# First feed-forward's gate vector: from TensorE products at the kernel's begin to weight rows on VectorE, GpSimd and ScalarE behind the first two tiles

## The chip, the cores and the metric

One core of a Trainium2 chip runs the whole program. The metric is the device time of one execution in microseconds (us); less is better. Timed runs are given by their median; one further execution was profiled, and the trace rows are from that one.

## What is computed

The model is a two-layer backbone over 768 tokens (256 context, 512 latent) of width 1024. Each layer has a feed-forward, a mixer and a second feed-forward, each with an adaLN modulation (shift, scale, gate) that is a matrix product with the conditioning vector:

```python
mod   = (silu(c)     @ w_mod + b_mod).reshape(1, 1, 9, 1024)     # for the latent tokens
mod_c = (silu(c_ctx) @ w_mod + b_mod).reshape(1, 1, 9, 1024)     # for the context tokens
h, gt = pre_mod(x, mod, norm_g, 0)       # h = rms_norm(x) * g * (1 + scale) + shift; gt = gate
x  = x  + 0.5 * gt  * swiglu(h,  w_gu, w_down)
xc = xc + 0.5 * gtc * swiglu(hc, w_gu, w_down)
```

The change concerns `gt` and `gtc` of the first feed-forward of layer 0: piece 2 of nine, 1024 columns of `w_mod`, for two vectors (`c` and `c_ctx`).

## The kernel before, in words

All of it is float32 work. A product is made of three TensorE products of halves: a weight tile `raw` is split by ScalarE into a rounded `whi` (line 128, a copy) and by VectorE into the rest `wlo` (line 129, a subtraction); activations have the same two halves (`hh`, `hl`). Tokens lie in the free dimension, so a gate is one number per partition and 128-column block.

The tile framework orders the instructions of each engine when it builds the program: a list schedule by readiness, with program order as the priority. Each engine then runs its queue strictly in that order. `keep_in_program_order` ties an instruction behind the one that was traced before it on its engine; other instructions may still be put between. Pools are taken from the left or right end of SBUF like stacks; with `reuse_waits="tile"` a new tile that covers the place of old ones waits for those tiles alone.

The begin. SP issues nearly all loads in one queue. `first_load` brings 1 MB tiles `m` (tag `m0`, 4 buffers) of `w_mod0a`: eight tiles with shift and scale of one 128-block each, then four tiles with the gate's columns. `first_product` multiplies a tile with silu(c) on TensorE (line 208, 16 instructions), ScalarE copies the row out (line 211), and four small products (line 214) turn it into columns; VectorE adds the bias (lines 221 to 224, for the gate line 230). Each of the eight shift and scale tiles lets `norm_apply` make one 128-block k of `h` (lines 348 to 351).

Meanwhile TensorE works on the first two tiles of the hidden layer, f = 0 and 1 (line 506, in the order k, f): 192 matmuls in three PSUM tiles. Then `up` takes them out (SiLU on ScalarE, product with the PSUM half on VectorE, split). f = 2 and 3 follow with `pair` (line 375). From f = 4 on a Strassen-like scheme with seven half-size products per tile is used (`unit`, line 607, matmuls of 384 columns). It needs sums of blocks of `h`: `seven_open` makes them on VectorE (lines 577 and 565), four times for k = 0 to 3: sums in two buffers `tt`, and from these the split tiles `t` (T1, T2, T4; eight tiles in the pool `tsum`, on the right side, 36 KB of each partition) and `t3`, later split into h (T3). Each `unit` also makes weight sums on VectorE (line 629) and splits them; these halves are named S1 to S4 here. The other modulation pieces are made later by `mod_step` from weight rows on VectorE (line 298, one row tile `wm` of 128x512 for two instructions), with silu of the conditioning row, broadcast over the partitions, in `cb` (lines 276 and 277).

The right side holds first the pool `w2` (the split weights of f = 0 and 1, 32 KB), which is closed after the two tiles; `tsum` takes its place. The gate `mod[0][2]` is first used at line 401 after six hidden tiles.

Of the kernel before, what the change touches and what calls it, by code (L numbers as in the profile page):

```python
# [8 lines left out]
F32 = mybir.dt.float32  # L9
F32R = mybir.dt.float32r  # L10
BF16 = mybir.dt.bfloat16
I32 = mybir.dt.int32
U8 = mybir.dt.uint8
AF = mybir.ActivationFunctionType
ALU = mybir.AluOpType
# [3 lines left out]
D = 1024  # L19
KT = D // 128  # L20
# [27 lines left out]
class Net:  # L48
# [146 lines left out]
        nc.vector.reduce_sum(self.four, self.ident.rearrange("p (j v) -> p v j", j=4)[:, 0:2, :], axis=AX.X)  # L195

    def first_load(self, m, pool):
        raw = pool.tile([128, KT, 256], F32, tag="m0", name="m0", bufs=4)
        self.nc.sync.dma_start(out=raw, in_=self.ins["w_mod0a"][m])
        return raw  # L200

# [21 lines left out]
        nc.vector.tensor_scalar(out=sc, in0=scale, scalar1=b[:, KT + m:KT + m + 1], scalar2=1.0, op0=ALU.add, op1=ALU.add)  # L223
        nc.vector.tensor_scalar(out=sc, in0=sc, scalar1=self.ng[0][:, 0, m:m + 1], scalar2=None, op0=ALU.mult)

    def first_gate(self, pool, i, raw):

        for j, x in enumerate(self.first_product(pool, raw)):
            m = 2 * i + j
            self.nc.vector.tensor_scalar(out=self.mod[0][2][:, m, :], in0=x, scalar1=self.bmod[0][:, 2 * KT + m:2 * KT + m + 1],  # L230
                                         scalar2=0.5, op0=ALU.add, op1=ALU.mult)

    def first_stats(self, pool):

# [222 lines left out]
    def ffn(self, l, sub, idx, segs, nxt, bg=(0, 0), first=4, start=False):  # L457
        nc = self.nc
        gate = self.mod[l][3 * sub + 2]
        gu = self.ins[f"gu{l}{idx}"]  # L460

        w2s = ExitStack()
        w2 = self.pool("w2", w2s, side="right")
        early = 2
        w = {}
        for f in range(2):
            w[f] = self.load_split(gu[f], 2048, w2)
            yield False
        h = yield True
        st = ExitStack()  # L470
        with st:
            pool = self.pool("ffn", st)
            hid = {}

            def hidden(f):
                hid[f] = (pool.tile([128, T], F32R, tag="dh", name="dh", bufs=6),
                          pool.tile([128, T], F32R, tag="dl", name="dl", bufs=6))

            def up(f, ss, regs=None):

                if not regs:
                    regs = self.regions(ss)
                    self.pair(w[f], KT, h, ss, regs)
                if f not in hid:
                    hidden(f)
                sg = pool.tile([128, T], F32, tag="sg", name="sg", bufs=1)
                for reg, (s0, s1) in zip(regs, ss):
                    nc.scalar.activation(out=sg[:, s0:s1], in_=reg[0], func=AF.Silu)
                    nc.vector.tensor_tensor(out=sg[:, s0:s1], in0=sg[:, s0:s1], in1=reg[1], op=ALU.mult)
                a, b = ss[0][0], ss[-1][1]  # L490
                self.split(sg[:, a:b], hid[f][0][:, a:b], hid[f][1][:, a:b])

            main = [(0, CTX), (CTX, T)] if segs[0][0] == 0 else [(CTX, T)]
            if start:

                a = [self.psum_a() for _ in range(3)]
                a = a[1:] + a[:1]
                for f in range(2):
                    nc.tensor.matmul(out=a[2][:, f, :], lhsT=self.zero[:, 0:128], rhs=self.zero, start=True, stop=False)
                regs = [[[a[2][:, f, j * 256:(j + 1) * 256] for j in range(2)], [a[f][:, j, :] for j in range(2)]]  # L500
                        for f in range(2)]
                for f, k in [(f, k) for k in range(KT - 2) for f in range(2)] + [(f, KT - 2 + k) for f in range(2) for k in range(2)]:
                        for j in range(2):
                            for i, (wi, xi) in enumerate(((0, 0), (0, 1), (1, 0))):
                                for s, (s0, s1) in enumerate(main):
                                    nc.tensor.matmul(out=regs[f][s][j], lhsT=w[f][j][wi][:, k * 128:(k + 1) * 128],
                                                     rhs=h[k][xi][:, s0:s1], start=(s == 1 and k == 0 and i == 0),
                                                     stop=(k == KT - 1 and i == 2 and s + j > 0))
                for f in range(2):
                    up(f, main, regs[f])  # L510
            else:
                for seg in segs:
                    for f in range(early):
                        up(f, [seg])
                    if seg == segs[0]:
                        w[early] = self.load_split(gu[early], 2048)
                        up(early, [seg])
            w2s.close()
            sts = ExitStack()
            seven_start, seven = self.seven_open(sts, h, segs[0][0])  # L520
            if not start:
                up(early, [(segs[1][0], T)])
                early += 1
            for pi, (f0, nf) in enumerate(PARTS):
                for f in range(f0, f0 + nf):
                    if f >= early:
                        if f >= first:
                            if f == first:
                                sp = seven_start()
                                if self.pending:  # L530
                                    self.mod_open(self.pool("modp", sts, side="right"))
                            hidden(f)
                            sg = pool.tile([128, T], F32, tag="sg", name="sg", bufs=1)
                            seven(sp, gu[f], sg, hid[f])
                        else:
                            w[f] = self.load_split(gu[f], 2048)
                            up(f, main)
                    if f >= first:
                        self.mod_step(bg[0])
                xk = [hid[f] for f in range(f0, f0 + nf)]  # L540
                dn = self.ins[f"dn{l}{idx}_{nf}"][pi % 2 if nf == 6 else pi - 2]
                load = lambda u: self.load_split(dn[u], 2 * nf * 128)
                if pi == len(PARTS) - 1:
                    self.mod_step(1000)
                    sts.close()
                    self.psum_open()
                    h = self.close_out(load, nf, xk, segs, gate, nxt)
                else:
                    for u in range(4):
                        wd = load(u)  # L550
                        regs = self.regions(main)
                        self.pair(wd, nf, xk, main, regs)
                        self.add_gated(regs, u, main, gate)
                        self.mod_step(bg[1])
        yield h
# [1132 lines left out]
def build(tc, ins, outs, stages=("ffn1_0", "pair", "ffn2_0", "ffn1_1", "gla", "ffn2_1")):  # L1688
    with ExitStack() as ctx:
        n = Net(tc, ctx, ins, outs)  # L1690
# [11 lines left out]
        with ExitStack() as st:  # L1702
            pool = n.pool("start", st)
            l, sub, segs = first[stages[0]]
            h = n.h_new()
            n.first_open(pool)
            n.x_move(ins["x_t"], False, [(0, T)])
            if stages[0] == "ffn1_0":
                raw = {}
                for m in range(2):  # L1710
                    raw[m] = n.first_load(m, pool)
                    gens[0].early()
                with tc.high_priority():
                    bc = n.first_stats(pool)
                for m in range(2):
                    n.first_norm(pool, m, raw[m])
                for m in range(KT):
                    if m > 1:
                        n.first_norm(pool, m, n.first_load(m, pool))
                    for s0, s1 in ((0, CTX), (CTX, T)):  # L1720
                        n.norm_apply(pool, 0, 0, (s0, s1), bc[:, s0:s1], m, h)
                for i in range(4):
                    n.first_gate(pool, i, n.first_load(KT + i, pool))
            else:
                for m in range(KT):
                    n.first_norm(pool, m, n.first_load(m, pool))
                n.mod_queue(*[(0, p) for p in range(2, 9)], *[(1, p) for p in range(9)])
                with tc.tile_pool(name="mm", bufs=1) as mp:
                    n.mod_open(mp)
                    n.mod_step(1000)  # L1730
                gens[0].early(9)
                for seg in segs:
                    n.norm_mod(pool, l, sub, seg, h)
# [114 lines left out]
```

## Time and profile before

| | |
|---|---|
| Timed runs, median of 3 (lowest to highest) | 2703.78 us (2703.27 to 2707.57) |
| Profiled execution | 2706.87 us, of which the span of the profile is 2705.1 us |
| Mean granted TensorE clock | 0.991 of full speed |
| Busy in the span | TensorE matmul 97%, VectorE 80%, ScalarE 44%, GpSimd 6% |

The span runs from the first to the last instruction that the profile shows. PE is TensorE, PEld its weight loads, DVE VectorE, ACT ScalarE, POOL GpSimd, SP the engine that issues the DMAs. An engine's busy share is a mean over stages; what a microsecond is worth is read from the stage it is in.

### The profile page before, as it was taken

The numbers are of one execution on the slowest core, as the hardware profiler recorded it, in microseconds if no ns is written. First come the engines' busy times: TensorE is split into PE (matmuls) and PEld (weight loads), VectorE is DVE, ScalarE is ACT, GpSimd is POOL, SyncE is SP. The second block draws the span as 40 slices with busy tenths as digits, with TensorE's granted clock in tenths as the row PEclk, the third lists the DMA queues.
The fourth block names the chain that finished last, engine by engine and source line by source line (L and its number), as shares of the span: only waits on it lengthen the run. The fifth ranks groups of instructions, "written<-read, shape, count | busy, mean of one in ns | idle before, by whom it ended". The sixth has DMA issues, their size and how long they took to land. (4 is left out here: it accounts for less than half of the span.)

```text
span 2705.1 us, 44031 instructions
## 1 busy us (share of the span) xinstructions
PE 2616.4 (97%) x16800; PEld 2433.8 (90%) x16800; DVE 2163.0 (80%) x4503; ACT 1197.2 (44%) x2254; POOL 171.6 (6%) x206
## 2 busy tenths in 40 slices
PE   7999999999879899999999999999999999999999
PEld 5899999989767789999999899999998998989898
DVE  6789798977888867797988878888777777768777
ACT  4324242445757744242424542424345565435344
POOL 0000000013543200000000000000000121000000
PEclk9999999999989999999999999999999999999999
DMA  8143444331000140434343314343232111422333
GB/s 314 42 150 115 139 133 144 122 128 42 24 24 1 44 144 28 129 113 129 118 140 100 117 63 137 104 147 107 93 109 92 60 67 63 148 71 92 105 106 125
DMA packets 103572, 279.31 MB, mean 103 GB/s; under 512 B 12256, under 2 KB 15200, under 8 KB 101824
## 3 DMA queue, kind: packets, MB, share of 16 engines
q1 hardware_dynamic: 103360, 276.50, 31.5%
q8 instruction: 132, 2.16, 0.3%
q14 instruction: 80, 0.66, 0.1%
HBM read 269.11 MB, written 7.34 MB: 102 GB/s over the span
## 5 line engine op out<-in xcount | busy, mean ns | idle before, releaser
L128 ACT ACTIVATE whi<-raw 128x512 fp32r<-128x512 f32 (+3 forms) x466 | 355.5, 767 | 740.5 <-PE r L375 331.3
L129 DVE TENSOR_TENSOR wlo<-raw,whi 128x512 fp32r<-128x512 f32 (+3 forms) x466 | 401.0, 863 | 81.8 <-ACT whi L128 78.7
L607 PE MATMUL r<-t,whi 128*128 128x384 f32 (+1 forms) x1704 | 400.8, 323 | 1.5 <-DVE u L644 0.9
L607 PE MATMUL r<-hh,wlo 128*128 128x384 f32 (+1 forms) x1136 | 366.0, 322 | 0.0
L607 PE MATMUL r<-hh,whi 128*128 128x384 f32 (+1 forms) x1136 | 365.8, 322 | 0.0
L607 PE MATMUL r<-hl,whi 128*128 128x384 f32 (+1 forms) x1136 | 365.8, 322 | 0.0
L298 DVE SCALAR_TENSOR_TENSOR junk<-wm,cb 128x512 bf16<-128x512 f32 x480 | 329.5, 686 | 12.7 <-ACT cb L277 7.7
L607 PEld LDWEIGHTS r<-t,whi 128*128 128x128 f32 x1704 | 295.7, 188 | 2.8 <-DVE u L644 1.8
L607 PE MATMUL r<-t,wlo 128*128 128x384 f32 (+1 forms) x852 | 273.3, 323 | 0.0
L375 PE MATMUL r<-dh,whi 128*128 128x512 f32 (+1 forms) x952 | 267.4, 346 | 0.8 <-ACT whi L128 0.8
L375 PE MATMUL r<-dh,wlo 128*128 128x512 f32 (+1 forms) x952 | 266.7, 346 | 0.3 <-DVE wlo L129 0.3
L375 PE MATMUL r<-dl,whi 128*128 128x512 f32 (+1 forms) x952 | 266.8, 344 | 0.0
L128 ACT ACTIVATE whi<-s 128x512 fp32r<-128x512 f32 x284 | 174.7, 625 | 180.9 <-DVE s L629 67.3
L607 PEld LDWEIGHTS r<-hl,whi 128*128 128x128 f32 x1136 | 213.4, 188 | 0.8
L607 PEld LDWEIGHTS r<-hh,wlo 128*128 128x128 f32 x1136 | 213.4, 188 | 0.4 <-DVE wlo L129 0.4
L607 PEld LDWEIGHTS r<-hh,whi 128*128 128x128 f32 x1136 | 213.3, 188 | 0.3
L375 PEld LDWEIGHTS r<-dh,wlo 128*128 128x128 f32 x952 | 178.6, 188 | 24.4 <-DVE wlo L129 1.1
L375 PEld LDWEIGHTS r<-dh,whi 128*128 128x128 f32 x952 | 178.0, 188 | 24.5 <-ACT whi L128 2.7
L375 PEld LDWEIGHTS r<-dl,whi 128*128 128x128 f32 x952 | 178.1, 188 | 23.4
L129 DVE TENSOR_TENSOR wlo<-s,whi 128x512 fp32r<-128x512 f32 x284 | 190.9, 685 | 3.8 <-ACT whi L128 3.2
L401 DVE SCALAR_TENSOR_TENSOR x<-r,mod,x 128x512 f32<-128x512 f32 (+1 forms) x168 | 100.1, 632 | 90.9 <-PE r L375 90.5
L607 PEld LDWEIGHTS r<-t,wlo 128*128 128x128 f32 x852 | 159.9, 188 | 0.1
(417 smaller groups left out, 5847.3 us busy)
## 6 DMA issues: line engine op xcount, KB each, us to landing
raw<-gu SPq DMA_DIRECT2D x176, 512.0 KB, 3.8
wm<-w_mod SPq DMA_DIRECT2D x240, 256.0 KB, 2.9
raw<-dn SPq DMA_DIRECT2D x88, 320.0 KB, 3.0
raw<-dn SPq DMA_DIRECT2D x64, 384.0 KB, 3.1
raw<-w_out SPq DMA_DIRECT2D x28, 512.0 KB, 3.9
m<-w_mod0a SPq DMA_DIRECT2D x12, 1024.0 KB, 10.3
raw<-w_in SPq DMA_DIRECT2D x8, 512.0 KB, 4.9
raw<-w_kq SPq DMA_DIRECT2D x8, 512.0 KB, 3.6
```

The costliest lines, as they stand in the source:

```text
L128: self.nc.scalar.activation(out=hi, in_=src, func=AF.Copy)
L129: (e or self.nc.vector).tensor_tensor(out=lo, in0=src, in1=hi.bitcast(F32), op=ALU.subtract)
L298: nc.vector.scalar_tensor_tensor(out=junk, in0=w, scalar=1.0, in1=self.cb[:, v, :], op0=ALU.mult, op1=ALU.mult, accum_out=self.acc[:, m, v ...
L375: m = nc.tensor.matmul(out=outs[s][j], lhsT=w[j][wi][:, k * 128:(k + 1) * 128], rhs=xk[k][xi][:, s0:s1], start=(k == 0 and i == 0), stop=( ...
L401: self.nc.vector.scalar_tensor_tensor(out=self.xs[m][:, s0:s1], in0=regs[s][j], scalar=gate[:, m, v:v + 1], in1=self.xs[m][:, s0:s1], op0= ...
L607: nc.tensor.matmul(out=o, lhsT=y[wi], rhs=x[k][xi], start=first and k == 0 and i == 0, stop=last and k == H - 1 and i == 2, skip_group_che ...
```

## The change

The four gate products at the begin go away: no `first_load` of the four gate tiles, no `first_product` on them, no line 230. `m0` has 3 buffers in place of 4, and a pool `gate` (19 KB of each partition) is opened on the right side ahead of `w2`. After the first two hidden tiles `first_gate` computes the same vector: silu of both conditioning rows, broadcast; then for each of the eight 128-blocks m and both halves i of the contraction a 256 KB row tile `w` (3 buffers), one VectorE multiply with sum for `c`, one GpSimd multiply for `c_ctx`, and one ScalarE copy with sum over GpSimd's product. `mod_finish` adds the bias and the factor 0.5. The VectorE, ScalarE and SP instructions are tied behind the ones traced before them.

```diff
     def first_load(self, m, pool):
-        raw = pool.tile([128, KT, 256], F32, tag="m0", name="m0", bufs=4)
+        raw = pool.tile([128, KT, 256], F32, tag="m0", name="m0", bufs=3)
...
+    def first_gate(self, pool, l=0, p=2):
+        nc, H, keep = self.nc, D // 2, self.tc.keep_in_program_order
+        cb = [pool.tile([128, 2, H], F32, name=f"gc{i}") for i in range(2)]
+        for i in range(2):
+            for v in range(2):
+                src = self.ins["c_row"][v:v + 1, i * H:(i + 1) * H]
+                keep(nc.sync.dma_start(out=cb[i][:, v, :], in_=src.to_broadcast([128, H])))
+        for i in range(2):
+            keep(nc.scalar.activation(out=cb[i], in_=cb[i], func=AF.Silu))
+        acc = [pool.tile([128, KT, 2], F32, name=f"ga{i}") for i in range(2)]
+        for m in range(KT):
+            for i in range(2):
+                w = pool.tile([128, H], F32, tag="gw", name="gw", bufs=3)
+                keep(nc.sync.dma_start(out=w, in_=self.ins[f"w_mod{l}"][p * KT + m][:, i * H:(i + 1) * H]))
+                junk = pool.tile([128, H], BF16, tag="gj", name="gj", bufs=1)
+                keep(nc.vector.scalar_tensor_tensor(out=junk, in0=w, scalar=1.0, in1=cb[i][:, 0, :], op0=ALU.mult,
+                                                    op1=ALU.mult, accum_out=acc[i][:, m, 0:1]))
+                t = pool.tile([128, H], F32, tag="gt", name="gt", bufs=2)
+                nc.gpsimd.tensor_tensor(out=t, in0=w, in1=cb[i][:, 1, :], op=ALU.mult)
+                keep(nc.scalar.activation(out=t, in_=t, func=AF.Copy, accum_out=acc[i][:, m, 1:2]))
+        nc.vector.tensor_tensor(out=self.mod[l][p], in0=acc[0], in1=acc[1], op=ALU.add)
+        self.mod_finish(l, p)
...
-        w2s = ExitStack()
+        gs, w2s = ExitStack(), ExitStack()
+        if start:
+            gp = self.pool("gate", gs, side="right")
         w2 = self.pool("w2", w2s, side="right")
...
                 for f in range(2):
                     up(f, main, regs[f])
+                w2s.close()
+                self.first_gate(gp)
+                gs.close()
...
-                for i in range(4):
-                    n.first_gate(pool, i, n.first_load(KT + i, pool))
```

## Rows read from the trace of the kernel before

**Rows 1.** The page's first part: busy us, share, instructions of each engine.

```profile
PE 2616.4 (97%) x16800; PEld 2433.8 (90%) x16800; DVE 2163.0 (80%) x4503; ACT 1197.2 (44%) x2254; POOL 171.6 (6%) x206
```

**Rows 2.** Stretches: from:to length, busy of PE PEld DVE ACT POOL, PE clock, DMA, GB/s.

```profile
57.81:82.80 24.99, 24.99 (x175) 18.38 (x175) 6.28 (x18) 3.27 (x8) 0.00 (x0) 1.00 0.03 12
...
80.79:121.42 40.63, 40.63 (x235) 36.27 (x234) 35.45 (x57) 18.09 (x30) 0.00 (x0) 1.00 0.14 46
```

**Rows 3.** Timeline of PE around a gate product: start, duration, instruction.

```profile
63.10 0.63 PE L208 MATMUL b<-m,silu_T 128*32 128x256 f32 x6
63.66 0.61 PE L214 MATMUL b<-four,m0r 128*128 128x2 f32 x4
64.19 1.05 PE L208 MATMUL b<-m,silu_T 128*32 128x256 f32 x10
65.18 0.62 PE L506 MATMUL a<-hh,whi 128*128 128x256 f32 x2
```

**Rows 4.** Timeline of PE, first matmuls of f = 2, f = 4, and the fourth product.

```profile
82.80 0.28 PE L375 MATMUL b<-hh,whi 128*128 128x256 f32 x1
...
116.25 0.33 PE L607 MATMUL r<-hh,whi 128*128 128x384 f32 x1
...
122.48 0.34 PE L607 MATMUL r<-hh,whi 128*128 128x384 f32 x1
```

**Rows 5.** Timeline of DVE, in brackets idle time before and its releaser.

```profile
80.79 1.82 DVE L577 TENSOR_TENSOR tt<-hh,hl 128x768 f32<-128x768 f32 x2
...
90.79 0.95 DVE L129 TENSOR_TENSOR dl<-sg,dh 128x768 fp32r<-128x768 f32 x1
...
93.73 1.14 DVE L565 TENSOR_TENSOR tt<-tt 128x384 f32<-128x384 f32 x2
...
119.20 0.69 DVE L129 TENSOR_TENSOR wlo<-raw,whi 128x512 fp32r<-128x512 f32 x1 [2.50 <-ACT whi L128]
...
120.74 0.68 DVE L129 TENSOR_TENSOR wlo<-s,whi 128x512 fp32r<-128x512 f32 x1
```

**Rows 6.** Timeline of ACT, the first split of a sum and silu of cb.

```profile
83.70 0.53 ACT L128 ACTIVATE t<-tt 128x384 fp32r<-128x384 f32 x1 [0.55 <-DVE tt L565]
...
117.59 1.06 ACT L277 ACTIVATE cb<-cb 128x1024 f32<-128x1024 f32 x1 [2.21 <-DMA cb<-c_row]
```

**Rows 7.** Timeline of DVE, two row products of the later modulation.

```profile
163.35 0.69 DVE L298 SCALAR_TENSOR_TENSOR junk<-wm,cb 128x512 bf16<-128x512 f32 x1
...
164.09 0.69 DVE L298 SCALAR_TENSOR_TENSOR junk<-wm,cb 128x512 bf16<-128x512 f32 x1
```

**Rows 8.** Groups by form on POOL and ACT: count, busy us, mean ns, idle before.

```profile
L1008 POOL TENSOR_TENSOR qa<-qa,rs 128x512 f32<-128x512 f32 x6 | 6.2, 1062 | 1.4 <-DVE rs L151 1.4
...
L1091 ACT ACTIVATION_READ_ACCUMULATOR pr<-s,nm 128x1 f32 x96 | 19.6, 204 | 0.0
```

**Rows 9.** Timeline of DVE and POOL together, in the mixer of layer 0.

```profile
797.13 2.05 POOL L1008 TENSOR_TENSOR qa<-qa,rs 128x512 f32<-128x512 f32 x2 [0.20 <-DVE rs L151]
...
798.14 0.28 DVE L1095 TENSOR_TENSOR pt<-t,pt 128x128 fp32r<-128x128 f32 x1
...
804.13 0.28 DVE L707 TENSOR_TENSOR qa<-ra,rb 128x128 f32<-128x128 f32 x1
804.28 2.09 POOL L1008 TENSOR_TENSOR qa<-qa,rs 128x512 f32<-128x512 f32 x2 [0.66 <-DVE rs L151]
804.33 1.14 DVE L708 TENSOR_TENSOR qa<-rb,ra 128x128 f32<-128x128 f32 x1
```

**Rows 10.** DMA: m tiles (KB each, us to landing); landing of row tiles wm.

```profile
m<-w_mod0a SPq DMA_DIRECT2D x12, 1024.0 KB, 10.3
...
DMA to landing us min/median/max: 2.4/2.9/5.3
```

**Rows 11.** Timeline of PE, 256-column matmuls early and ten us later.

```profile
31.29 0.41 PE L506 MATMUL a<-hh,whi 128*128 128x256 f32 x1
...
41.92 0.28 PE L506 MATMUL a<-hh,wlo 128*128 128x256 f32 x1
```

More of the change, by code (lines that the diff above doesn't have):

```diff
@@ L224, in first_norm @@
         nc.vector.tensor_scalar(out=sc, in0=sc, scalar1=self.ng[0][:, 0, m:m + 1], scalar2=None, op0=ALU.mult)
[L226 to L231, printed above, removed]
+    def first_gate(self, pool, l=0, p=2):
[20 more added lines that the diff above has]
+        self.mod_finish(l, p)
     def first_stats(self, pool):
```

## The prediction

> **What bounds the kernel now.** I read the busy shares first, then the waits, then the begin on the timeline, engine by engine. TensorE is busy for 97% of the span [rows 1], so what counts is whether TensorE gets its next operand in time. From 57.81 to 82.80 us, the second half of the first two tiles, it is busy without a gap, and the four gate products lie in there; DMA is nearly silent (0.03) and VectorE mostly idle (6.28 of 24.99 us busy) [rows 2]. A microsecond of TensorE work removed there is a microsecond saved there. From 80.79 to 121.42 TensorE is gapless too, but now VectorE is busy 35.45 of 40.63 us [rows 2]: it makes the sums T1 to T4 and the first weight sums, which the Strassen products at 116.25 and after want [rows 4]. The reader is to see that the change takes work from an engine that has none to spare there, and puts work on another one just where that has little to spare.
>
> I call E the end of line 506, 82.80 before [rows 4], and count from it.
>
> **What is removed.** Between two line 506 matmuls one gate costs TensorE 63.10 to 65.18 us, 2.08 us: sixteen line 208 matmuls in two lots and four of line 214 [rows 3]. The restart of the stream adds something; I take 0.1. Four gates: 4 x 2.2 = 8.8 us (8.3 with no restart cost, 9.1 with 0.2). Their loads (4 MB) end before this stretch [rows 2], the line 211 copies and line 230 adds sit on idle engines: nothing more is saved. E moves to 74.0.
>
> **m0 with three buffers.** Each of the eight remaining tiles is asked for one product later. DMA share is 0.03 after 57.81 [rows 2], and four tiles of 1 MB no longer stand in the queue: I take 0; without that cover it is a tile's landing, 10.3 us in the full queue of before [rows 10].
>
> **What is added on SP and DMA.** Twenty issues: four broadcasts of 256 KB and sixteen rows of 256 KB. The first seven are queued behind the last m tile and land under line 506. The other thirteen wait for a buffer. Behind a waiting issue in SP's queue stand the weights of f = 4 and 5, loaded long ahead; a row lands 2.9 us after its issue [rows 10].
>
> **What is added on VectorE.** The first multiply is tied behind the last VectorE instruction of `up(1)`, at 90.79 before, 8 us after E [rows 5]; the new silu is tied in the same way on ScalarE. So the idle VectorE time ahead of E is out of reach, and all sixteen fall in the busy stretch. Two such instructions start 0.74 us apart, accumulator read included [rows 7]: 16 x 0.74 = 11.8 us, and four small adds, estimated at 0.2, give 12.6 us.
>
> **What is added on GpSimd.** Sixteen 128x512 multiplies; the nearest rows have 1.06 us each [rows 8], 16 x 1.06 = 17.0 us. The question is whether they run beside VectorE. At 804.13 a 128x128 VectorE instruction with both inputs in SBUF takes 0.28 us; the like one at 804.33, just after GpSimd began a 1.04 us multiply, takes 1.14, GpSimd's time more. At 798.14 one whose input is in PSUM takes 0.28 under a running GpSimd multiply [rows 9]. So a GpSimd multiply and a VectorE instruction with two SBUF inputs exclude each other. Nearly all VectorE work of this stretch has two SBUF inputs (lines 577, 565, 129, and the new multiplies). Bounds: 0 if every multiply finds VectorE waiting anyway, 17.0 if none does. VectorE will be the late engine with hardly a gap, so I take 16.6, sixteen at the 1.04 of the undisturbed case.
>
> The Trainium skill (SBUF — State Buffer, Who interferes with whom) says it as a rule: a VectorE instruction with two SBUF inputs contends with a GpSimd instruction that reads SBUF, and the later one blocks fully. This trace agrees (0.28 to 1.14 us [rows 9]); by a reading in which the engines do not disturb each other the 16.6 us would be 0.
>
> **What is added on ScalarE.** Two silus at 1.06 [rows 6] and sixteen copies with sum, each about 0.63 (a copy of 384 columns takes 0.53 [rows 6]) and 0.20 for the sum [rows 8]: 15.4 us. It is busy 18 of 40.63 us [rows 2]; I take 0 of its own. Its splits get later by up to one copy, 0.8 us, a few times.
>
> **Where the stall goes.** `tsum` lies where `w2` was: its first split runs at 83.70, once line 506 is through [rows 6]. Now the gate pool lies at the outer end of the right side and `tsum` (36 KB) covers it too (19 KB): by the order of allocation the tile t11 and all of k = 2 and 3 wait for gate tiles that are read up to the last row. So the sums cannot overtake the gate; they follow it.
>
> The last operand with little slack is S3: its rest is made at 120.74 to 121.42 [rows 5], TensorE wants it at 122.48 [rows 4]: slack 1.1 us. VectorE idles 40.63 - 35.45 = 5.2 us on the way [rows 2], of which 2.5 wait for the silu of cb [rows 5], whose load waits for the place of the sums and comes again; 2.7 can be filled. TensorE is late by 12.6 + 16.6 - 2.7 - 1.1 = 25.4 us. Nothing later gives it back, TensorE having no gaps.
>
> **Sum:** 25.4 - 8.8 = +16.6 us. The span of 2705.1 becomes 2721.7; the execution around it, 2706.87, becomes 2723.5. That execution lay 3.1 us over the median of the runs, so for the median: 2703.8 + 16.6 = 2720.4, say 2720 us. Against no change, 0.2% (5.4 us) is about what a measurement of this kernel tells.
>
> Unknown, for the range: after such a stall the clock. Matmuls of 256 columns took 0.41 us at 31.29, after mostly waiting, and 0.28 at 41.92 [rows 11], the levels of 1.2 and 2.4 GHz. Some 3 to 4 us at the lower level would cost about 2 us, if VectorE isn't the limit then anyway.
>
> **The rivals.**
>
> *GpSimd hides, the waits remain.* If GpSimd runs beside VectorE, three row buffers set the pace: per three rows a landing of 2.9, a multiply of 1.06 and some 0.4 of hand-over, 1.45 us a row, 23 us for sixteen. The gate ends 31 us after E; then one leftover of 1.5, and k = 2 and 3 at 2 x 0.91 + 4 x 0.57 + 1.5 = 5.6 us of VectorE each [rows 5] with some waits, T3 and the weight sums 4: S1 at E + 48.5. Before, TensorE wanted it one product after 116.25, (122.48 - 116.25) / 3 = 2.1 us [rows 4], so at E + 35.5. Late by 13, net +4 to +6: 2709 us. For it: VectorE idles between rows. Against it: [rows 9].
>
> *Only VectorE's own work counts.* No wait for places, no block by GpSimd: 12.6 - 2.7 - 1.1 = 8.8 late, net 0: 2704.
>
> *Rows come too late.* A buffer is free only when both multiplies are done. If the three come free together, three rows take 3 x 1.8 + 2.9 + 0.3 = 8.6 us rather than 5.4, 46 us in all, 17 more: 2737. For it: in the sum a row is wanted 2 x 1.8 = 3.6 us after its buffer is free, and landing takes 3.2. Against it: they come free one by one.
>
> *Faster.* The multiplies are in truth spread so that the sums are done by the time TensorE asks; the whole 8.8 us stay: 2695. For it: `first_gate` isn't wanted until after six tiles, far behind. It decides if VectorE is late by less than the 3.8 us that it can fill, which four of the sixteen rows alone use up; against it stands the tie behind `up(1)` with program order as priority.
>
> **How the numbers follow.** Forecast 0.53 (2715 to 2726). GpSimd hides 0.20, of this 0.16 beyond 0.2% slower and 0.04 within, since it ends at the bound and any latency adds. Rows too late 0.13. VectorE's own work alone 0.08, within. Faster 0.06. Slower 0.53 + 0.16 + 0.13 = 0.82, same 0.12, faster 0.06. The range 2708 to 2733 leaves out faster, the same of 2704 and the upper half of the late rows, 0.2.
>
> **What would show it.** E at 74 (72 to 76) and no line 208 after the eighth tile. The gate's VectorE multiplies start 7 to 9 us after E and end some 28 us later. GpSimd multiplies or VectorE's line 577, 565 and 129 instructions are stretched beyond their 1.06, 0.91 and 0.57 us. No split into `t` for k = 2 and 3 before the last row. TensorE has a gap of 20 us and more ahead of the first Strassen products or in f = 3, ended by VectorE. Wrong would be: a gap under 9 us (then faster); VectorE durations unchanged (then the first rival); VectorE idle with row loads as the releaser (the third).

## The result and the profile after

The kernel with the change takes 2725.86 us (median of 6 runs, 2724.17 to 2731.32), the kernel before, on the same chip, 2705.91 us (6 runs, 2703.27 to 2708.24). The ratio is 1.0078 (95% interval 1.0068 to 1.0089): 20 us slower, where 2720 was forecast (16.6 us slower). The profiled execution has a span of 2726.5 us.

The page's first part, which answers to [rows 1]; the columns are busy us, share and instructions of each engine:

```profile
PE 2611.6 (96%) x16720; PEld 2435.2 (89%) x16720; DVE 2185.6 (80%) x4531; ACT 1208.1 (44%) x2284; POOL 199.7 (7%) x222
```

TensorE does less and the program takes longer, so TensorE must wait somewhere. Its timeline shows what is gained and what is lost, beside [rows 4]:

```profile
73.64 0.28 PE L393 MATMUL b<-hh,whi 128*128 128x256 f32 x1
...
107.54 0.34 PE L630 MATMUL r<-hh,whi 128*128 128x384 f32 x1
...
109.45 0.34 PE L630 MATMUL r<-hh,wlo 128*128 128x384 f32 x1
136.31 1.01 PE L630 MATMUL r<-t,whi 128*128 128x384 f32 x2 [26.52 <-ACT whi L128]
```

E, the end of line 506 and first matmul of f = 2, is at 73.64 and not at 82.80: 9.16 us gained. The first Strassen product, the only one that needs no sum, begins 8.7 us sooner too. Then TensorE stands for 26.52 us until a weight sum is split: the second product needs T1 and S1. The stretches from E to past the gap, with the columns of [rows 2]:

```profile
73.64:112.52 38.88, 36.15 (x205) 31.46 (x203) 35.04 (x48) 20.23 (x47) 27.81 (x16) 1.00 0.31 102
112.52:137.00 24.48, 0.69 (x2) 0.50 (x2) 22.98 (x41) 9.45 (x17) 0.00 (x0) 0.50 0.03 7
137.00:140.00 3.00, 3.00 (x11) 2.97 (x11) 1.90 (x3) 0.50 (x1) 0.00 (x0) 0.58 0.96 266
```

In the first stretch VectorE and GpSimd work on the gate; in the second GpSimd is silent, VectorE works through the sums with hardly a pause (busy 22.98 of 24.48 us), and TensorE has work only at the very end. The third column from the right is the granted clock: 0.50 (1.2 GHz) in the gap, 0.58 in the three microseconds after it.

What the gate's tiles did, one row tile `gw` and the products `gt` (duration min/median/max in ns, first and last start):

```profile
L243 DVE SCALAR_TENSOR_TENSOR gj<-gw,gc x16: 691/1550/1776, 80.5 to 111.9; 128x512 bf16<-128x512 f32 x16
L246 POOL TENSOR_TENSOR gt<-gw,gc x16: 1417/1744/2268, 80.5 to 109.8; 128x512 f32<-128x512 f32 x16
...
DMA to landing us min/median/max: 2.4/2.6/6.9
```

VectorE's multiply, 0.69 us in [rows 7], has a median of 1.55; GpSimd's, some 1.04 in [rows 9], 1.74. On VectorE's timeline the last multiply, with no GpSimd instruction left beside it, is back at 0.69, and the first sum's rest follows it:

```profile
84.48 2.30 DVE L129 TENSOR_TENSOR wlo<-raw,whi 128x1024 fp32r<-128x1024 f32 x1
...
110.11 1.75 DVE L243 SCALAR_TENSOR_TENSOR gj<-gw,gc 128x512 bf16<-128x512 f32 x1
...
111.90 0.69 DVE L243 SCALAR_TENSOR_TENSOR gj<-gw,gc 128x512 bf16<-128x512 f32 x1
...
113.28 0.55 DVE L129 TENSOR_TENSOR t<-tt,t 128x384 fp32r<-128x384 f32 x1
...
134.03 0.96 DVE L129 TENSOR_TENSOR t<-tt,t 128x768 fp32r<-128x768 f32 x1 [0.91 <-ACT t L128]
134.91 0.68 DVE L652 TENSOR_TENSOR s<-raw 128x512 f32<-128x512 f32 x1
```

And ScalarE: the first split of a sum into `t` (k = 0, both parts in one row) stands right behind the gate's last copy. Before, it ran 0.9 us after E [rows 6]; now 38.3 us after it.

```profile
111.34 0.63 ACT L247 ACTIVATE gt<-gt 128x512 f32<-128x512 f32 x1 [0.82 <-POOL gt L246]
111.88 0.19 ACT L247 ACTIVATION_READ_ACCUMULATOR gt<-gt 128x1 f32 x1
111.97 1.24 ACT L128 ACTIVATE t<-tt 128x384 fp32r<-128x384 f32 x2
...
133.16 0.84 ACT L128 ACTIVATE t<-tt 128x768 fp32r<-128x768 f32 x1 [1.48 <-DVE tt L588]
```

So the order of events is: gate from E + 6.8 to E + 39.0, then the rest of the sums and their splits for all four k in 21.6 us (113.28 to 134.91), then the first weight sums, then TensorE. Nearly the whole loss is in this one stage: the first instruction of line 401 (now line 419), which follows it, is 20.2 us late, the last one of the kernel 21.4. The first one on VectorE's timeline, before and after:

```profile
154.49 0.75 DVE L401 SCALAR_TENSOR_TENSOR x<-r,mod,x 128x512 f32<-128x512 f32 x1 [2.15 <-PE r L375]
174.71 0.75 DVE L419 SCALAR_TENSOR_TENSOR x<-r,mod,x 128x512 f32<-128x512 f32 x1 [2.15 <-PE r L393]
```

### The profile page after: what moved, and what is told of

Its sections match the earlier page's. It is cut to its first block, busy times and chain, and to the rows that moved or that the text cites. A ratio compares the mean times of both kernels' runs of the same rounds, so it can differ in the third digit from the quotient of the medians.

```text
span 2726.5 us, 43999 instructions
## 1 busy us (share of the span) xinstructions
PE 2611.6 (96%) x16720; PEld 2435.2 (89%) x16720; DVE 2185.6 (80%) x4531; ACT 1208.1 (44%) x2284; POOL 199.7 (7%) x222
## 5 line engine op out<-in xcount | busy, mean ns | idle before, releaser
L630 PE MATMUL r<-t,whi 128*128 128x384 f32 (+1 forms) x1704 | 402.2, 324 | 28.5 <-ACT whi L128 26.5
```

The lines of the kernel that those rows point to most:

```text
L630: nc.tensor.matmul(out=o, lhsT=y[wi], rhs=x[k][xi], start=first and k == 0 and i == 0, stop=last and k == H - 1 and i == 2, skip_group_che ...
```

## The experiments

In all of them E is the first matmul of f = 2, the gate's end is the end of its last multiply or copy, and the gap is TensorE's longest wait of the stage. In the kernels without any TensorE gate E lies between 70.67 and 75.34 us, so one profiled execution is uncertain by some 2 us from the begin alone; differences in us are worked out from the ratio of the timed runs and 2706 us. Beside them the kernel before had medians of 2707.29 us (e1, e2, e3, e7), 2705.10 (e4 to e6) and 2706.82 (e8 to e10).

**Without any row** (e3). It leaves out the sixteen rows with all their loads, multiplies and copies: the gate is bias alone.

```diff
+        for i in range(2):
+            nc.vector.memset(acc[i], 0.0)
-        for m in range(KT):
-            for i in range(2):
-                w = pool.tile([128, H], F32, tag="gw", name="gw", bufs=3)
-                keep(nc.sync.dma_start(out=w, in_=self.ins[f"w_mod{l}"][p * KT + m][:, i * H:(i + 1) * H]))
...
```

> Leaves out all rows: no loads, no multiplies, the gate is its bias alone. What is left of the change is the TensorE work removed at the begin. If that work was on the path and nothing else is late: -8 to -9.5 us (first matmul of f = 2 at 73.6 in place of 82.8). If VectorE's sums were the real limit ahead of the Strassen products, only the 3.8 us that VectorE had to fill count: -4.

2698.0 us (7 runs), ratio 0.9967 (0.9956 to 0.9978), -9 us. TensorE has no gap. What TensorE gives up (8.8 us forecast) is worth its full time within the interval (6 to 12 us), and the three `m0` buffers cost nothing that shows.

**Without the context row** (e2). It leaves out the GpSimd multiply and ScalarE's copy; VectorE's sixteen multiplies stay.

```diff
-                t = pool.tile([128, H], F32, tag="gt", name="gt", bufs=2)
-                nc.gpsimd.tensor_tensor(out=t, in0=w, in1=cb[i][:, 1, :], op=ALU.mult)
-                keep(nc.scalar.activation(out=t, in_=t, func=AF.Copy, accum_out=acc[i][:, m, 1:2]))
```

> Leaves out the context vector's multiply and sum (GpSimd and ScalarE), so that the gate of the context tokens is its bias alone. Exclusion: a row costs VectorE 0.735, or the three buffers set the pace, (2.6 landing + 0.3 issue + 0.7) / 3 = 1.2 us a row, 20 us for sixteen in place of 32: 12 us less, +7 to +9 us over before. If GpSimd's work were hidden beside VectorE: at most 2 us less than the change, +18 to +20.

2714.36 us (6 runs), ratio 1.0027 (1.0016 to 1.0039), +7 us. Its row tiles, in the view used above:

```profile
L245 DVE SCALAR_TENSOR_TENSOR gj<-gw,gc x16: 680/692/694, 81.7 to 102.1; 128x512 bf16<-128x512 f32 x16
...
  DMA gw<-w_mod: 5.0, 4
```

Without GpSimd beside it the multiply takes 0.69 us, all sixteen of them. So the context row was the cause of the stretching. The edit takes out ScalarE's copies too, but they are not it: in the change the multiply at 111.90 takes 0.69 us while ScalarE works (111.97) and GpSimd does not. What is left is GpSimd. The sixteen rows still take 21 us, since VectorE now waits four times for a row (5.0 us); the gap is 15.2 us.

**Without VectorE's row** (e7). The reverse: it leaves out VectorE's multiply, GpSimd and ScalarE do their part.

```diff
-                junk = pool.tile([128, H], BF16, tag="gj", name="gj", bufs=1)
-                keep(nc.vector.scalar_tensor_tensor(out=junk, in0=w, scalar=1.0, in1=cb[i][:, 0, :], op0=ALU.mult,
-                                                    op1=ALU.mult, accum_out=acc[i][:, m, 0:1]))
```

> Leaves out VectorE's row multiply (the latent tokens' gate is its bias alone); GpSimd and ScalarE do the context row as in the change. If GpSimd's time on the rows and the wait for the gate's places count: GpSimd runs at 1.04 to 1.3 us a row, buffers set (2.6 + 0.3 + 1.1) / 3 = 1.35, sixteen end some 22 to 24 us after their start in place of 32: +10 to +12 us over before. If only VectorE's own 12.6 us of rows made the change slow: -5 to 0.

2721.44 us (4 runs), ratio 1.0053 (1.0036 to 1.007), +14 us, with a gap of 21.0 in the profiled execution, the fastest of the four (2716.35). The median is more than I expected (10 to 12), though the interval reaches down to +10, and VectorE's timeline shows something that my sum had no place for:

```profile
80.07 1.23 DVE L129 TENSOR_TENSOR wlo<-raw,whi 128x1024 fp32r<-128x1024 f32 x1 [2.58 <-ACT whi L128]
88.12 1.15 DVE L129 TENSOR_TENSOR wlo<-raw,whi 128x512 fp32r<-128x512 f32 x1 [6.83 <-ACT whi L128]
...
91.95 1.79 DVE L129 TENSOR_TENSOR dl<-sg,dh 128x768 fp32r<-128x768 f32 x1 [1.76 <-ACT dh L128]
98.67 0.64 DVE L129 TENSOR_TENSOR hl<-t,hh 128x384 fp32r<-128x384 f32 x1 [4.92 <-ACT hh L128]
```

While GpSimd multiplies (77.5 to 104.2 with ScalarE's last copy), VectorE is nearly idle (6.2 us busy from 77.0 to 104.2); it could make most of the sums, and doesn't. Its time was not what the sums waited for here.

**Both vectors on VectorE** (e1). The whole gate, GpSimd and ScalarE relieved of it.

```diff
-                nc.gpsimd.tensor_tensor(out=t, in0=w, in1=cb[i][:, 1, :], op=ALU.mult)
-                keep(nc.scalar.activation(out=t, in_=t, func=AF.Copy, accum_out=acc[i][:, m, 1:2]))
+                for v in range(2):
...
+                    keep(nc.vector.scalar_tensor_tensor(out=junk, in0=w, scalar=1.0, in1=cb[i][:, v, :], op0=ALU.mult,
+                                                        op1=ALU.mult, accum_out=acc[i][:, m, v:v + 1]))
```

> The changed kernel with the context vector's multiply done by VectorE too, in place of GpSimd and ScalarE. If GpSimd's multiplies and VectorE's two-input instructions exclude each other, a row costs 1.73 us in the changed kernel (0.69 + 1.04 in turn) and 2 x 0.735 = 1.47 here: 16 x 0.26 = 4 us less, +15 to +17 us over before against the +20 measured for the change. If the two engines run beside each other and only VectorE's own work counts, it is 16 x 0.735 = 12 us more: about +31.

2725.65 us (4 runs), ratio 1.0069 (1.0052 to 1.0086), +19 us: the same as the change within the intervals, and nearer to what was expected if the two engines exclude each other (15 to 17) than to the rival (31). But the 4 us less than the change that I expected with it did not come.

```profile
L244 DVE SCALAR_TENSOR_TENSOR gj<-gw,gc x32: 681/691/694, 80.1 to 112.4; 128x512 bf16<-128x512 f32 x32
```

Thirty-two undisturbed multiplies on one engine last 33 us; sixteen on each of two engines that block one another last 32 us (80.45 to 112.60). As a second engine GpSimd brought nothing that shows here.

**The place held, nothing multiplied** (e6). It leaves out all multiplies; one tile as large as the gate's pool (19 KB) is kept busy by a chain of ten small loads, each followed by a 0.2 us copy of one column.

```diff
+        w = pool.tile([128, 4896], F32, name="hold")
+        seen = pool.tile([128, 1], F32, name="seen")
+        for m in range(10):
+            keep(nc.sync.dma_start(out=w[:, 0:H], in_=self.ins[f"w_mod{l}"][p * KT + m % KT][:, 0:H]))
+            keep(nc.scalar.activation(out=seen, in_=w[:, 0:1], func=AF.Copy))
```

> Leaves out all sixteen row multiplies (the gate's sums are zeros). In their place one 19 KB tile lies in the gate pool, and a chain of ten 256 KB loads into it, each followed by a tiny ScalarE copy, holds its place: a link is a landing (2.4 to 2.9 us for a row tile) and some 0.5 us of hand-over, so the hold ends about 38 us after E (E: the first line 375 matmul) with VectorE, GpSimd and ScalarE free all the time. Theory (the place decides when the sums follow; the multiplies matter by how long they hold it): the splits into t come after the hold, the last one some 21 us behind it, TensorE has a gap of about 25 us, and the time is that of the change, +15 to +20 us against before. Rival (what counts is the engine time that the multiplies take from VectorE and GpSimd, and the place only shifts work that has slack): no gap of over 5 us, -9 to -4 us like the kernel without any rows.

2721.13 us (4 runs), ratio 1.0056 (1.0041 to 1.0072), +15 us. ScalarE's timeline:

```profile
105.04 0.20 ACT L234 ACTIVATE seen<-hold 128x1 f32<-128x1 f32 x1 [2.16 <-DMA hold<-w_mod]
107.88 0.20 ACT L234 ACTIVATE seen<-hold 128x1 f32<-128x1 f32 x1 [2.63 <-DMA hold<-w_mod]
107.98 1.25 ACT L128 ACTIVATE t<-tt 128x384 fp32r<-128x384 f32 x2
112.56 0.52 ACT L128 ACTIVATE t<-tt 128x384 fp32r<-128x384 f32 x1 [2.58 <-DVE tt L575]
```

And TensorE's:

```profile
131.57 1.01 PE L617 MATMUL r<-t,whi 128*128 128x384 f32 x2 [20.35 <-ACT whi L128]
```

No engine has more to do for the gate than ten copies of 0.2 us, and the sums wait all the same until the last copy. The hold ends 33.0 us after E and not 38, and the gap is 20.4 us and not 25. The rival, engine time, asked for a gain of 4 us and more. It has fallen.

**The same hold in another place** (e8). Like e6, but the held tile (8 KB) lies between the buffers `tt` and the pool `tsum`, apart from the `w2` tiles by a filler of 4 KB, so that no T tile covers it.

```diff
         w2 = self.pool("w2", w2s, side="right")
+        if start:
+            self.pool("pad", gs, side="right").tile([128, 1024], F32, name="pad")
+            gp = self.pool("gate", gs, side="right")
-        w = pool.tile([128, 4896], F32, name="hold")
+        w = pool.tile([128, 2064], F32, name="hold")
```

> The kernel of e6 (all row multiplies left out, ten chained loads and ten tiny ScalarE copies), with one difference: the held tile lies between the sums' buffers and the pool tsum, where no T tile covers it. Theory (the wait for a place is what holds the sums): the splits into t run as in the kernel without rows, no TensorE gap, -8 to -10 us against before. Rival (the splits stand behind the chain's copies in ScalarE's queue, or SP's queue is what is late): a gap of about 20 us as in e6, +15 to +20 us.

2701.42 us (10 runs), ratio 0.9981 (0.9972 to 0.999), -5 us, 20 us less than e6. ScalarE's timeline:

```profile
74.40 1.25 ACT L128 ACTIVATE t<-tt 128x384 fp32r<-128x384 f32 x2
79.94 0.53 ACT L128 ACTIVATE t<-tt 128x384 fp32r<-128x384 f32 x1 [0.80 <-DVE tt L576]
81.29 0.19 ACT L234 ACTIVATE seen<-hold 128x1 f32<-128x1 f32 x1
...
107.56 0.20 ACT L234 ACTIVATE seen<-hold 128x1 f32<-128x1 f32 x1 [1.88 <-DMA hold<-w_mod]
```

The chain is as long as in e6 and ends at the same time, but the sums run ahead of it from 0.3 us after E. The place, and not the chain's loads or copies, held them. Less was gained than expected (-8 to -10): TensorE still has two small waits, ended by VectorE, and E is at 74.14, 2.7 us later than in e3.

```profile
115.63 0.41 PE L618 MATMUL r<-hh,whi 128*128 128x384 f32 x1 [1.18 <-DVE sg L497]
123.76 0.62 PE L618 MATMUL r<-t,whi 128*128 128x384 f32 x2 [1.43 <-DVE u L655]
```

**Half the hold** (e10). e6 with `range(5)` for `range(10)`.

> The kernel of e6 with five chained loads in place of ten (all row multiplies left out). In the runs so far the TensorE gap was the time from E to the end of the gate (or of the hold) less 12.5 us (10.7 to 14.7 in seven runs). Theory: five links of 2.95 us less, so the hold ends 18 us after E, the gap is about 6 us (4 to 8), and the time -5 to +1 us against before. Rival (the gap does not follow the place one for one): a gap over 12 us or none.

2709.84 us (10 runs), ratio 1.0015 (1.0006 to 1.0024), +4 us: 3 us over what I expected. The gap is 8.3 us, just above the 4 to 8 that I expected, and the clock after it is 0.50 for some microseconds here too.

**Half the gate on rows, ahead of `up`** (e4). Blocks 0 to 3 stay on TensorE (two tiles), blocks 4 to 7 become eight rows with both vectors on VectorE, not tied there.

```diff
-        for m in range(KT):
+        for m in range(4, KT):
...
+                self.first_gate(gp)
+                with self.tc.high_priority():
                     for f in range(2):
                         up(f, main, regs[f])
```

> Computes the whole gate: 128-blocks 0 to 3 by two TensorE tiles at the begin as before, blocks 4 to 7 by eight row tiles with both vectors on VectorE (16 x 0.735 = 11.8 us), and these multiplies are traced ahead of up and not tied on VectorE, with up at high priority. VectorE idles about 13 us between 50 us and E in the trace of the change. Theory (the same work costs nothing where VectorE idles, and the loss came from its place behind up and ahead of the sums): E moves by 2 x 2.29 = 4.6 us, the sums come in time, -3 to -5 us against before. Rival (the rows come too late for the idle time, or the place of the gate pool holds the sums in any case): part of the rows falls behind E, 0 to +8 us.

2714.13 us (5 runs), ratio 1.0034 (1.0021 to 1.0047), +9 us. A miss, and just above the rival's 0 to +8. ScalarE's timeline:

```profile
63.64 0.39 ACT L211 ACTIVATE m0r<-b 128x256 f32<-128x256 f32 x1 [4.27 <-PE b L208]
...
68.42 0.38 ACT L211 ACTIVATE m0r<-b 128x256 f32<-128x256 f32 x1 [3.30 <-PE b L208]
75.17 0.60 ACT L516 ACTIVATE sg<-a 128x512 f32<-128x512 f32 x1 [6.37 <-PE a L534]
75.67 2.00 ACT L236 ACTIVATE gc<-gc 128x1024 f32<-128x1024 f32 x2
```

The silus of the conditioning rows (line 236) stood in ScalarE's order behind the row copies of the two remaining TensorE gates (line 211) and behind the first SiLU of `up` (line 516), to which the edit had given priority and which waited 6.37 us for TensorE. They ran at 75.67, so that the multiplies began at 76.75 and the pool was held to 98.8. The idle time of VectorE was not used, and the gap is 9.0.

**All rows ahead of `up`** (e5). The same with sixteen rows and no TensorE gate.

> Computes the whole gate from sixteen row tiles with both vectors on VectorE (32 x 0.735 = 23.5 us), traced ahead of up and not tied on VectorE, with up at high priority. About 13 us of idle VectorE time lie ahead of E, so some 10 us of multiplies spill behind E; VectorE can fill about 4 us there. Theory: E moves by 9.2 us, TensorE gets a gap of 5 to 10 us, -6 to +3 us against before. Rival (the position ahead of up does not help, since rows arrive at the pace of their three buffers and the pool's place is held to the last row): as the change, +12 to +18 us.

2719.22 us (5 runs), ratio 1.005 (1.0036 to 1.0063), +14 us: the theory (-6 to +3) missed, and the time is the rival's. Two multiplies ran at 64.65; the others were ordered behind the first product of `up`, at 70.53, and the last ended at 105.6. The gap is 19.7.

**Half the gate on rows, in a free place** (e9). The whole gate again. The loads are held back until the scale of block 4 is there, the silus come before block 7's row copy, the sixteen multiplies are tied behind the last block of h and ahead of the two TensorE gates' columns; the rows lie in the begin's pool or between `tt` and `tsum`, and of the T tiles only t00 covers anything, the first of the two conditioning tiles.

```diff
+                raw = [n.first_load(KT + i, pool) for i in range(2)]
+                gs = ExitStack()
+                n.first_gate(pool, n.pool("ga", gs, side="right"), n.pool("gb", gs, side="right"))
+                gs.close()
                 for i in range(2):
-                    n.tile_gate(pool, i, n.first_load(KT + i, pool))
+                    n.tile_gate(pool, i, raw[i])
```

> Computes the whole gate: blocks 0 to 3 by two TensorE tiles at the begin, blocks 4 to 7 by eight rows with both vectors on VectorE, tied behind the last block of h and ahead of up, with their tiles in places that no T tile needs after E (the rows in the begin's pool). Theory: the 11.8 us of multiplies fit into VectorE's idle time before E or spill by 1 to 2 us, the gate ends at E or before, no TensorE gap, and two gates of 2.3 us are saved: -3 to -5 us against before. Rival (the VectorE and ScalarE work in the begin delays the last blocks of h or the first sums): E later than 79 or a gap of 2 us and more, -1 to +4 us.

2703.78 us (11 runs), ratio 0.9987 (0.9978 to 0.9995), -3.5 us (-6 to -1.4). VectorE's timeline, first and last multiply and the first sum:

```profile
64.01 0.69 DVE L246 SCALAR_TENSOR_TENSOR gj<-gl,gc 128x512 bf16<-128x512 f32 x1
...
76.51 0.69 DVE L246 SCALAR_TENSOR_TENSOR gj<-gl,gc 128x512 bf16<-128x512 f32 x1
77.12 0.08 DVE L246 DVE_READ_ACCUMULATOR gj<-gl,gc 128x1 f32 x1
77.24 0.17 DVE L249 TENSOR_TENSOR mod<-ga,ga 128x8 f32<-128x8 f32 x1
77.32 1.82 DVE L605 TENSOR_TENSOR tt<-hh,hl 128x768 f32<-128x768 f32 x2
```

E is at 76.72; the rows end 0.5 us after it, and TensorE's longest wait of the stage is 0.5 us. It beats the kernel before and the changed one, the former by little: less than the 0.2% that I named as what a measurement tells, though the interval of 11 runs lies below 1. Against e4 it has another order of the silus and multiplies as well as another place; what each of the two gave was not separated.

**All runs together.** The gap follows the gate's end wherever the gate lies under the T tiles:

| | gate or hold ends, us after E | gap, us | difference |
|---|---|---|---|
| e10, half the hold | 18.3 | 8.3 | 10.0 |
| e4, half ahead | 19.7 | 9.0 | 10.7 |
| e2, VectorE's rows alone | 27.6 | 15.2 | 12.4 |
| e5, all ahead | 31.8 | 19.7 | 12.1 |
| e6, place held | 33.0 | 20.4 | 12.6 |
| e7, GpSimd's rows alone | 33.5 | 21.0 | 12.5 |
| the change | 39.0 | 26.5 | 12.5 |
| e1, both on VectorE | 39.5 | 25.4 | 14.1 |
| e8, hold elsewhere | 33.6 | none over 1.4 | |
| e9, rows before E | 0.5 | none over 0.5 | |

Each microsecond by which the gate ends later than some 10 to 14 us after E is about a microsecond of gap, whichever engines do it, or none. The difference can be read from the change: TensorE has 36.2 us of work from E that needs no sum (36.15 busy in the first stretch above), and from the gate's end to the first matmul that needs one 23.7 us pass (112.60 to 136.31). The gap is 39.0 + 23.7 - 36.2 = 26.5 us. In the other seven TensorE has 35.7 to 36.2 us of such work, and between 22.1 (e1) and 26.2 us (e10) pass after the gate.

## Why the prediction was right in its size and in part wrong in its reason

*What is removed.* Forecast 8.8 us, measured 9.16 at E: right; e3 (-9 us, -12 to -6) shows that it reaches the end.

*The position.* The first multiply was forecast 7 to 9 us after E and came 6.8 after it; the tie behind `up(1)` did what was said. The rows did not spread out, so the rival "faster" has fallen.

*GpSimd and VectorE exclude each other.* Right. The signs named ahead are all there: the multiply stretched to 1.55, the 1024-column rest to 2.30, a 384-column rest to 1.64. The Trainium skill (SBUF — State Buffer, Who interferes with whom) states that the later of the two blocks fully; e2 against the change (0.69 to 1.55 us) agrees. The rival "GpSimd hides" asked for unchanged durations and has fallen. The price was somewhat too high: the sixteen multiplies took 21.1 us in place of 11.0 (e2), and the four two-input instructions between them (line 129 at 84.48, 93.93, 99.78 and 108.55) some 1.08 us more each than in e1, 14.4 us in all where 16.6 was forecast; five of the sixteen multiplies took 0.69 and were not held up. Nor do [rows 9] show quite "GpSimd's time more": from 0.28 to 1.14 us is 0.86, beside a multiply of 1.04. The gate was forecast at some 28 us and lasted 32.1, with those four instructions between and 2.4 us of waiting for rows.

*Where the stall goes.* Right that the sums cannot overtake the gate and follow it, and that the covered place decides it; e6 and e8 show it. Two things failed. First, I held that only t11 and k = 2 and 3 would wait. k = 0 waited as well: its splits stand behind the gate's last copy in ScalarE's order although by the order of allocation t00 and t10 cover no gate tile, and in e8 the same splits stand ahead of the copies. So what is shown is that a covered place puts the sums behind the gate; how much of that is a wait on the chip and how much the order that the list schedule made of it stays open. Second, and this is the step that was wrong, I priced the wait as VectorE's work: 12.6 + 16.6 - 2.7 - 1.1. That sum takes VectorE to be the late engine throughout. e7, where VectorE idles most of the gate's length and the gap is still 21.0, and e6, where it has no gate work at all and the gap is 20.4, show that the price is set by when the gate ends, whatever holds it. In the change the gate's 32.1 us are mostly VectorE's own multiplies and the time that GpSimd blocked it, the same two terms, and VectorE is busy 35.04 of 38.88 us up to the gate's end. That the sum came out near is in this respect luck: with idle engines it would have failed, as for e6. The operand that TensorE waited for was also an earlier one: S1's split for the second product, and not S3.

*The size.* TensorE was forecast 25.4 us late; from E to the first line 401 instruction it is 29.4 (20.2 + 9.16). In that stretch it waits 26.5 and once more 0.6 us, and is busy 2.3 us longer than before (73.92 us to 71.65). 1.6 of the 2.3 are the clock, named as unknown: from 136.31 to 139.44 nine matmuls took 3.13 us, at the 0.174 us of the product at 107.54 to 109.45 they take 1.57; I had said about 2. The other 2.4 us of the 4.0 over the forecast can't be put down to single terms: VectorE did not fill the 2.7 us of idle time (from E to 137.00 it idles 3.84 + 1.50 = 5.3 us, before 5.2 in a shorter stretch), but GpSimd's 16.6 was 2.2 too much.

*The other rivals.* Only VectorE's own work: fallen. Rows too late: fallen; VectorE waited 2.4 us for rows in the change, not 17, and without GpSimd (e2) 5.0.

## What to carry to other kernels

Work moved behind a stage takes the place of that stage's tiles as well as its engines: see which later tiles lie over the new ones before adding up engine time. Here the covered pool cost the whole time that it lived beyond some 10 to 14 us after E, even with idle engines. A chain of small loads that holds the place and computes nothing, in that place and beside it, separates the two in a pair of runs. And work for an idle stretch must have all its links there: here two silus that stood behind other work in ScalarE's order (e4) pushed the multiplies out of the stretch that was meant for them.

## What was not expected of the hardware

GpSimd's 128x512 multiply was slower than the nearest rows even without VectorE's: in e7 it has a median of 1.29 us, against some 1.04 to 1.06 in [rows 8, 9]. The two are not quite alike: line 1008 multiplies by a broadcast of eight values, the gate by a full row of 512. Whether that is the cause, or ScalarE's copies and the loads beside it, wasn't tried.

```profile
L245 POOL TENSOR_TENSOR gt<-gw,gc x16: 1283/1294/1747, 77.5 to 102.1; 128x512 f32<-128x512 f32 x16
```

The granted clock fell to 0.50 in a gap as short as that of e10 (8.3 us) and stayed there after the work came back. In e10, TensorE resumes at 119.81:

```profile
116.00:118.00 2.00, 0.00 (x0) 0.00 (x0) 1.09 (x3) 1.22 (x2) 0.00 (x0) 0.50 0.00 0
...
120.00:122.00 2.00, 2.00 (x7) 1.77 (x8) 1.97 (x4) 1.00 (x2) 0.00 (x0) 0.50 0.87 289
122.00:124.00 2.00, 2.00 (x8) 2.00 (x7) 0.41 (x1) 0.60 (x1) 0.00 (x0) 0.50 0.88 285
...
126.00:128.00 2.00, 2.00 (x13) 2.00 (x12) 1.91 (x4) 0.63 (x1) 0.00 (x0) 1.00 0.26 53
```

From 120 to 124 us fifteen matmuls ran at 0.50, where at 1.00 thirteen run in 2 us: some 1.7 us more than the gap itself went there, a part of what e10 lost beyond what I expected.
